# Paged decode attention beside an FFN: five small stages for two score pieces, and another order of buffers, copies and gathers

## The chip, the cores and the metric

The kernel runs on one core of a Trainium2 chip. The metric is the time of one execution on the device in microseconds (us); each kernel is given with the median of several runs. The program uses TensorE (PE in the profile, with PEld for its weight loads), VectorE (DVE), ScalarE (ACT), GpSimd (POOL) and SyncE (SP). SP only issues DMAs; POOL issues the gathers here.

## The reference, cut to what matters

One layer of a hybrid decoder runs over 512 prompt tokens and over 8 sample sequences of 4 new tokens, all with the same weights: an FFN, a mixer (a gated linear recurrence beside latent attention, 4 heads each), and a second FFN.

```python
h = h + 0.5 * rmsnorm(swiglu(rmsnorm(h, norm_g[0]), wg[0], wu[0], wd[0]), norm_g[1])
m, c_kv, k_r, s_fin = mixer(rmsnorm(h, norm_g[2]), ...)
h = h + rmsnorm(m, norm_g[3])
h = h + 0.5 * rmsnorm(swiglu(rmsnorm(h, norm_g[4]), wg[1], wu[1], wd[1]), norm_g[5])
```

The change touches the attention of the sample sequences over their cached keys. A sequence has 4,096 cached positions in pages of 128, which a page table names. A position has a latent row of 256 and a rotary row of 64 floats; the four heads share them. With 4 tokens by 4 heads there are 16 queries for each sequence:

```python
past_c = cache_kv_latent[l][page_table].reshape(Bs, past_len, KV_LORA)
past_r = cache_k_rope[l][page_table].reshape(Bs, past_len, QK_ROPE)
s = (jnp.einsum('bqhr,bsr->bhqs', ql, c_kv) + jnp.einsum('bqhd,bsd->bhqs', qr, k_rope)) * scale
p = jax.nn.softmax(jnp.where(k_pos <= q_pos, s, -jnp.inf), axis=-1)
o = jnp.einsum('bhqs,bsr->bqhr', p, c_kv)
```

## The kernel before

The 544 tokens are two parts: a (256 prompt tokens) and b (256 prompt tokens and the 32 sample tokens). Activations lie with features on the partitions. Every large product is made in three matmuls from a high and a low part of each operand (`gemm` L249, `mm3` L241, which holds L246). `weight` (L219) loads a block of 128 output columns on SP's queue into `wraw`, ACT casts it to the high part `wh` (L237), and DVE subtracts to get the low part `wl` (L238).

The stages in order are: FFN one on both parts, the mixer, and then the stretch that the change touches: the decode attention (the scope "dec", from L1022) interleaved with the second FFN of part a, the generator `gb` (L1019). Behind it come the output projection of part b, its second FFN (`gB`) and the last norms, with the rest of `gb` placed between them by `tail_a` (L1263) and the counts in `FILL` (L54).

`ffn` (L297) has 22 gate and up columns in four chunks; after each chunk it adds the chunk's share of the eight output columns ("down" columns). A unit, the work between two `yield`s, is one gate and up column (48 matmuls of 128x128 by 256 columns for part a) or one down column. There are 22 + 32 = 54 units. The halves `hha` and `hla` are the high and low parts of the chunk's hidden activations, written by ACT and DVE (L158, L159) and read by the down columns.

The decode attention works in 16 halves, two for each sequence (class `Half`, L1075). A half has two blocks of 1,024 cached positions: 1 MB of latent rows and 256 KB of rotary rows each, 8 rows to a partition. The steps of a half are:

- `gather` (L1081): two indirect DMAs on POOL's queue for each block. The latent rows go into one of six slots (`ulb`, `uhb`, `ha`, `hb`, `mb`, `q0`, the names under which the profile shows them), the rotary rows into one of four `rraw` buffers. Both blocks of a half are gathered at once.
- `turn` (L1100): DVE transposes 32x32 squares, three instructions a block (L1105 twice, 128x1024 each, L1106 for the rotary rows), into `kh` of 10 KB a partition, two buffers.
- `score` (L1109): 80 f32 matmuls on small tiles (64 rows by 32 columns) over ten feature columns, in two pieces of five columns (40 matmuls, L1118). They accumulate in two PSUM banks `s`, one for each r. Behind the second piece two reductions (L1125) and a maximum (L1127) give the greatest score of each row.
- `peak` (L1129): a matmul (L1131) spreads the maxima over the partitions; DVE reduces them and makes the bias of the exponential.
- `weigh` (L1138): two Exp on ACT, from PSUM to SBUF, with the row sums.
- `place` (L1143): a DVE transpose, and 16 small copies (32x64, L1149) into `pbuf`, 8 on DVE and 8 on ACT.
- `value` (L1151): 16 f32 matmuls (128 rows by 32 columns, L1157) of the weights with the gathered rows, straight behind the second score piece of a later half. After a sequence's second half the sums are copied to SBUF; `gathered` (L1163) adds up the four partition groups with two matmuls.

`decode` (L1171) puts these steps in thirds of a half: half n is gathered in its own turn, turned in turn n + 1, scored in turn n + 2, and its values follow in turn n + 3. The loop at the end of the scope takes one third, or one unit of `gb`, by a fixed ratio; in this way 43 of the 54 units fall into the decode:

```python
na, nb = NS + (NS + 2) // 3, int((22 + 32) * DRATE)
while ia < na:
    if ia * nb <= ib * na:
        next(ga, None)
        next(gn, None)
        ia += 1
    else:
        next(gb, None)
        ib += 1
```

`decode_new` (L1031) handles the new tokens' own keys between these steps. `decode_end` (L1210) combines the partial sums and makes the last products (L1243 is the matmul of the outputs); it also brings part b's mixer outputs back from DRAM on SP's queue.

PSUM has eight banks: four of tag "acc" for `gemm` and four of tag "ps", taken in turn, for all else (`ps`, L132). The order of the instructions on each engine is the order in which the code issues them.

Of the kernel before, what the change touches and what calls it, by code (L numbers as in the profile page):

```python
# [8 lines left out]
F32 = mybir.dt.float32  # L9
# [8 lines left out]
P = 128  # L18
# [3 lines left out]
NB = 8  # L22
# [27 lines left out]
NPS, PRT = {"ps": 4, "acc": 4, "pr": 1}, "ps"  # L50
# [3 lines left out]
FILL = (4, (7, 8, 9), (1, 2, 3, 4), 4)  # L54
# [5 lines left out]
DRATE = 0.8  # L60
KHB = 2
# [42 lines left out]
def hybrid_step_kernel(  # L104
# [27 lines left out]
    def ps(name, tag="ps"):  # L132
        return pp.tile([P, 512], F32, name=name, tag=tag, bufs=NPS[tag])
# [122 lines left out]
    def gemm_q(wt, act_):  # L256
# [3 lines left out]
        for k in range(kt):  # L260
            if k and k % 2 == 0:
# [35 lines left out]
    def ffn(i, n_post, xs, u, nxt=None, mid=None, late=None, fin=None, pre=()):  # L297
# [5 lines left out]
        for c, (f0, nf) in enumerate(FCH[i]):  # L303
            hh = {x: mk([P, FCH[i][0][1], HS[x]], F32R, "hh" + "ab"[x], pool=pool) for x in xs}
            hl = {x: mk([P, FCH[i][0][1], HS[x]], F32R, "hl" + "ab"[x], pool=pool) for x in xs}
            for j in range(nf):
                f = f0 + j
                wg_ = (w0 or [weight([wcols(w_g[i], 0, KD, f * P)], KD)]).pop(0)
                ga = {x: gemm(wg_, u[x]) for x in xs}
# [3 lines left out]
                up = {x: gemm(wu_, u[x]) for x in xs}  # L313
# [16 lines left out]
            for grp in groups:  # L330
                wts = {d: pre.pop(0) if pre else weight([wcols(w_d[i], f0, nf, d * P)], nf, len(grp) > 1) for d in grp}
                for x in xs:
                    for d in grp:
                        acc = gemm(wts[d], (hh[x], hl[x]))
# [18 lines left out]
                yield  # L353
# [665 lines left out]
    gb = ffn(1, 5, (0,), u4, late=lambda: rstd_u(u4[0], 0), pre=seam)  # L1019
    next(gb)  # L1020

    with scope("dec"):  # L1022
# [44 lines left out]
        slots = ("ulb", "uhb", "ha", "hb", "mb", "q0")  # L1067
# [3 lines left out]
        NS = 3 * NH2 + 11  # L1071

        PTG = {"ulb": 0, "uhb": -1, "ha": -1, "hb": 1, "mb": 0, "q0": -1}

        class Half:  # L1075
            def __init__(self, n):
                self.n, self.b, self.i = n, n // 2, n % 2
                self.bs = slice(self.b * 16, self.b * 16 + 16)
                self.p = pbuf[:, n % 2]

            def gather(self):  # L1081
                self.craw, self.rraw = [], []
                for g in range(2):
                    blk = 2 * self.n + g
                    slot = slots[blk % len(slots)]
                    if slot == "q0":
                        craw = qt
                    else:
                        craw = mk([P, ROWS * R + (256 if g == PTG[slot] else 0)], F32, slot, pool=act)
                    if g == PTG[slot]:  # L1090
                        self.pt = craw[:, ROWS * R :].rearrange("p (a k) -> p a k", a=ROWS)
                    craw = craw[:, : ROWS * R].rearrange("p (a r) -> p a r", a=ROWS)
                    rraw = mk([P, ROWS, RD], F32, "rraw", 4)
                    off = bass.IndirectOffsetOnAxis(ap=idx[:, blk : blk + 1], axis=0)
# [14 lines left out]
            def score(self, js):  # L1109
                q = qbd[self.b % 2]  # L1110
                if js[0] == 0:
                    self.s = [ps("s") for _ in range(2)]
# [319 lines left out]
```

## Time and profile before

| what | value |
|---|---|
| time, median of 3 runs (lowest, highest) | 1321.18 us (1320.61, 1322.22) |
| profiled execution: its own time | 1323.93 us |
| profiled execution: span, instructions | 1322.2 us, 30478 |
| mean granted TensorE clock in it | 0.994 |
| DVE, ACT, POOL busy | 887.5, 697.8, 76.7 us |
| DMA: moved, mean rate | 192.87 MB, 146 GB/s |

The profile is one execution. A busy time is the time in which an engine had an instruction in work. Matmuls overlap and their ends are modelled, so the busy share of PE is an upper bound of its use, and what PE really takes is read from the starts of instructions that follow each other. PEclk is the clock that the throttle granted, as a share of full speed. In a group's row, `out<-in` are the program's names; the last column is the time that the engine stood idle ahead of the group and the instruction that ended most of it ("issue": nothing that the profile shows). An order, shown in the prediction for both kernels, lists instructions of one engine in program order with the number of repeats; it has no times.

### The profile page before, as it was taken

The numbers are of one execution on the slowest core, as the hardware profiler recorded it, in microseconds if no ns is written. First come the engines' busy times: TensorE is split into PE (matmuls) and PEld (weight loads), VectorE is DVE, ScalarE is ACT, GpSimd is POOL, SyncE is SP. The second block draws the span as 40 slices with busy tenths as digits, with TensorE's granted clock in tenths as the row PEclk, the third lists the DMA queues.
The fourth block names the chain that finished last, engine by engine and source line by source line (L and its number), as shares of the span: only waits on it lengthen the run. The fifth ranks groups of instructions, "written<-read, shape, count | busy, mean of one in ns | idle before, by whom it ended". The sixth has DMA issues, their size and how long they took to land.

```text
span 1322.2 us, 30478 instructions
## 1 busy us (share of the span) xinstructions
PE 1284.7 (97%) x12696; PEld 1203.1 (91%) x12696; DVE 887.5 (67%) x1781; ACT 697.8 (53%) x1455; POOL 76.7 (6%) x80
## 2 busy tenths in 40 slices
PE   7999999999999999999999999999899999999998
PEld 6999999999999988889897887887787999999997
DVE  7553245434457787876867788989888868566664
ACT  7543244224456654445747665553455777554454
POOL 0000000000000000000000312313210000000000
PEclk9999999999999999999999999999899999999999
DMA  7223232233253313323332778968768645656451
GB/s 217 88 81 96 81 97 74 86 96 92 77 164 101 109 52 89 90 79 106 84 90 81 285 237 277 302 226 298 265 203 276 170 139 170 174 145 186 139 157 55
DMA packets 280552, 192.87 MB, mean 146 GB/s; under 512 B 12765, under 2 KB 271422, under 8 KB 275550
## 3 DMA queue, kind: packets, MB, share of 16 engines
q1 hardware_dynamic: 271920, 147.65, 38.7%
q0 software_dynamic: 7168, 41.95, 8.3%
q8 instruction: 100, 1.64, 0.5%
q10 hardware_dynamic: 1326, 1.32, 0.3%
q14 instruction: 38, 0.31, 0.1%
HBM read 181.22 MB, written 9.67 MB: 144 GB/s over the span
## 4 chain that ended last, share of the span: by engine, by line
PE 80%; DVE 10%; ACT 5%; issue 3%; DMA 2%; DVEq 0%; SPq 0%; ACTq 0%
PE acc L246 60%; PE acc L264 8%; DVE kh L1105 2%; PE s L1118 2%; DVE wl L238 2%; ACT wh L237 2%; PE s L922 1%; PE o L1157 1%; PE pa L661 1%; DMA wraw<-w_d 1%; PE zx L554 1%; ACT pbuf L1149 1%; DVE ssq L173 1%; PE pr L179 1%; DMA wraw<-w_g 0%
## 5 line engine op out<-in xcount | busy, mean ns | idle before, releaser
L237 ACT CAST wh<-wraw 128x1024 fp32r<-128x1024 f32 (+3 forms) x255 | 248.3, 976 | 318.1 <-PE acc L246 269.5
L238 DVE TENSOR_TENSOR wl<-wraw,wh 128x1024 fp32r<-128x1024 f32 (+3 forms) x255 | 288.3, 1132 | 140.1 <-ACT wh L237 139.4
L246 PE MATMUL acc<-uhb,wh 128*128 128x288 f32 x768 | 227.8, 297 | 0.8 <-ACT uhb L195 0.8
L246 PE MATMUL acc<-ulb,wh 128*128 128x288 f32 x768 | 227.2, 296 | 0.0
L246 PE MATMUL acc<-uhb,wl 128*128 128x288 f32 x768 | 225.7, 295 | 1.2 <-DVE wl L238 1.2
L246 PE MATMUL acc<-uha,wh 128*128 128x256 f32 x768 | 220.2, 287 | 2.1 <-DVE sil L318 1.0
L246 PE MATMUL acc<-uha,wl 128*128 128x256 f32 x768 | 217.2, 284 | 1.3 <-DVE wl L238 1.2
L246 PE MATMUL acc<-ula,wh 128*128 128x256 f32 x768 | 217.6, 284 | 0.6 <-DVE ula L196 0.6
L246 PEld LDWEIGHTS acc<-uha,wh 128*128 128x128 f32 x768 | 145.6, 190 | 6.7 <-issue 3.3
L246 PEld LDWEIGHTS acc<-uha,wl 128*128 128x128 f32 x768 | 145.4, 190 | 2.3 <-DVE wl L238 2.3
L246 PEld LDWEIGHTS acc<-ula,wh 128*128 128x128 f32 x768 | 145.7, 190 | 1.1 <-DVE ula L196 1.0
L246 PEld LDWEIGHTS acc<-uhb,wl 128*128 128x128 f32 x768 | 144.4, 188 | 1.7 <-DVE wl L238 1.7
L246 PEld LDWEIGHTS acc<-uhb,wh 128*128 128x128 f32 x768 | 144.1, 188 | 1.6 <-ACT uhb L195 1.0
L246 PEld LDWEIGHTS acc<-ulb,wh 128*128 128x128 f32 x768 | 144.2, 188 | 0.1
L246 PE MATMUL acc<-hhb,wh 128*128 128x288 f32 x317 | 93.5, 297 | 0.7 <-ACT hhb L158 0.7
L246 PE MATMUL acc<-hlb,wh 128*128 128x288 f32 x317 | 93.9, 297 | 0.1
L246 PE MATMUL acc<-hhb,wl 128*128 128x288 f32 x317 | 92.9, 294 | 0.0
L246 PE MATMUL acc<-hha,wh 128*128 128x256 f32 x297 | 87.4, 294 | 1.1 <-ACT hha L158 1.1
L246 PE MATMUL acc<-hla,wh 128*128 128x256 f32 x297 | 84.5, 284 | 1.1 <-DVE hla L159 1.1
L246 PE MATMUL acc<-hha,wl 128*128 128x256 f32 x297 | 84.5, 285 | 0.2 <-DVE wl L238 0.2
L321 DVE TENSOR_TENSOR sil<-sil,acc 128x256 f32<-128x256 f32 (+1 forms) x88 | 38.1, 435 | 49.7 <-PE acc L246 47.7
L320 DVE TENSOR_TENSOR sil<-sil,sit 128x256 f32<-128x256 f32 (+1 forms) x88 | 38.4, 440 | 45.0 <-ACT sit L295 44.7
(478 smaller groups left out, 2766.1 us busy)
## 6 DMA issues: line engine op xcount, KB each, us to landing
wraw<-w_g SPq DMA_DIRECT2D x66, 512.0 KB
wraw<-w_u SPq DMA_DIRECT2D x66, 512.0 KB
wraw<-w_in SPq DMA_DIRECT2D x24, 512.0 KB
wraw<-w_d SPq DMA_DIRECT2D x32, 384.0 KB
wraw<-w_d SPq DMA_DIRECT2D x32, 320.0 KB
wraw<-w_o SPq DMA_DIRECT2D x16, 512.0 KB
wraw<-w_d SPq DMA_DIRECT2D x16, 448.0 KB
wraw<-w_d SPq DMA_DIRECT2D x8, 512.0 KB
```

What stands on the lines that cost most here:

```text
L173: (eng or nc.vector).tensor_tensor(acc, acc, q, op=ALU.add)
L179: nc.tensor.matmul(pr[:, :n], ones, acc, start=True, stop=True)
L237: nc.scalar.copy(wh[:, :kt], w[:, :kt])
L238: nc.vector.tensor_tensor(wl[:, :kt], w[:, :kt], f32(wh[:, :kt]), op=ALU.subtract)
L246: nc.tensor.matmul(out, a, b, start=n == 0, stop=n == last)
L264: nc.tensor.matmul(acc[:, :n], a[:, k], b[:, k], start=k + i == 0, stop=k == kt - 1 and i == 2)
L320: nc.vector.tensor_tensor(s, s, t, op=ALU.mult)
L321: nc.vector.tensor_tensor(s, s, up[x], op=ALU.mult)
L554: nc.tensor.matmul(z, w[a][:, k], U[1][b][:, k], start=k + n == 0, stop=k == KD - 1 and n == 2)
L661: nc.tensor.matmul(pa[es, c * 32 : (c + 1) * 32].rearrange("p (n m) -> p n m", m=m), kx[:, cs], up(qx[:, cs]), start=True, stop=True, skip ...
L1105: nc.vector.transpose(kh[:, a : a + 4, :8].rearrange("p a j k -> p a (j k)"), self.craw[g][:, a : a + 4])
L1118: nc.tensor.matmul(self.s[r][c * 32 : c * 32 + 32, :P], q[rs, j], kh, start=j == 0, stop=j == 9, skip_group_check=True)
```

## The change

- A half is turned and scored in five stages of two feature columns, `JS`, the two rotary columns first. A stage takes 4 KB a partition in `kh` (three buffers) for both blocks: two DVE transposes of 128x512, and 16 score matmuls.
- The finished scores are copied from PSUM to SBUF (r = 0 by ACT, r = 1 by DVE) straight behind the last stage. One reduction over 128x256 replaces two and a maximum; Exp runs once, in place, from SBUF.
- `peak`, `weigh` and `place` are one step, in the next half's first stage. Of the 16 placing copies 4 are DVE's and 12 ACT's; the transposed weights have buffers of their own (`pt`).
- The values come in two runs of 8 matmuls, one for each block, in stages 3 and 4; behind each run one block is gathered, the rotary rows ahead of the latent rows. There is a seventh slot, `dx`.
- The eight PSUM banks are four "acc", two "ps" that only the scores hold in the decode, one "po" for the values and one "pm" for the maxima; other code takes the last three tags in the turn `CYC`.
- `ffn` with `fine=True` yields twice in each gate and in each up product (every 12 matmuls), and `gemm_2` makes all but the last k step of a chunk's first two down columns, then that step of both (in all chunks but the last). There are now 120 units; 100 of them go into the decode, beside one stage each time in a fixed ratio. `FILL` counts the finer units.
- By the order of SP's instructions the fetches of part b's mixer outputs and of `w_kv` in `decode_end` stand earlier, and two fetches of h later, behind the last values.

```diff
-NPS, PRT = {"ps": 4, "acc": 4, "pr": 1}, "ps"
+NPS, PRT = {"ps": 2, "po": 1, "pm": 1, "acc": 4}, "ps"
+CYC = ("ps", "po", "ps", "pm")
...
-FILL = (4, (7, 8, 9), (1, 2, 3, 4), 4)
+FILL = (13, (7, 8, 9), (1, 2, 3, 4), 4)
...
-DRATE = 0.8
-KHB = 2
+NDEC = 100
+JS = ((8, 9), (0, 1), (2, 3), (4, 5), (6, 7))
+KHB = 3
...
+    def gemm_2(wts, act_):
+        kt = wts[0][2]
+        n = act_[0].shape[-1]
+        accs = [ps("acc", "acc")[:, :n] for _ in wts]
+        for ks in (range(kt - 1), (kt - 1,)):
+            for (wh, wl, _), acc in zip(wts, accs):
+                for k in ks:
+                    for i, (a, b) in enumerate(((wh, act_[0]), (wh, act_[1]), (wl, act_[0]))):
+                        nc.tensor.matmul(acc, a[:, k], b[:, k], start=k + i == 0, stop=k == kt - 1 and i == 2)
+            if len(ks) > 1:
+                yield
+        return accs
...
-                ga = {x: gemm(wg_, u[x]) for x in xs}
+                ga, up = {}, {}
+                for x in xs:
+                    ga[x] = (yield from gemm_q(wg_, u[x], 4)) if fine else gemm(wg_, u[x])
+                if fine:
+                    yield
...
-        slots = ("ulb", "uhb", "ha", "hb", "mb", "q0")
+        slots = ("ulb", "uhb", "ha", "hb", "mb", "q0", "dx")
...
+            def turn(self, st):
+                kh = mk([P, 2, ROWS, 2, 32], F32, "kh", KHB)
+                j = JS[st][0]
                 for g in range(2):
...
+                    src = self.craw[g][:, :, j * 32 : j * 32 + 64] if j < 8 else self.rraw[g]
+                    nc.vector.transpose(kh[:, g].rearrange("p a j k -> p a (j k)"), src)
+                self.kh.append(kh)
...
-                mx = mk([P, 2], F32, "mxd", 2)
                 for r in range(2):
-                    nc.vector.tensor_reduce(mx[:, r : r + 1], self.s[r][:, :P], axis=AX.X, op=ALU.max)
+                    (nc.vector.tensor_copy if r else nc.scalar.copy)(self.e[:, r * P : r * P + P], self.s[r][:, :P])
                 self.mx = mk([P, 1], F32, "mxh", 2)
-                nc.vector.tensor_tensor(self.mx, mx[:, :1], mx[:, 1:], op=ALU.max)
+                nc.vector.tensor_reduce(self.mx, self.e, axis=AX.X, op=ALU.max)
...
-                        (nc.scalar.copy if g % 2 else nc.vector.tensor_copy)(self.p[g * 32 : g * 32 + 32, c // 2, c % 2 * 4 : c % 2 * 4 + 4, self.i * 16 : self.i * 16 + 16], src)
+                        (nc.scalar.copy if g else nc.vector.tensor_copy)(self.p[g * 32 : g * 32 + 32, c // 2, c % 2 * 4 : c % 2 * 4 + 4, self.i * 16 : self.i * 16 + 16], src)
...
+                for st in range(len(JS)):
                     if at(2):
-                        at(2).score(range(5, 10))
-                    if at(3):
-                        at(3).value(H.get(n - 4))
-                    if n >= 3 and at(0):
-                        at(0).gather()
-                    yield
...
+                        at(2).score(st)
+                    if n < 3 and st == 0:
+                        gather(2 + n // 2)
+                    if st == 0 and at(3):
+                        at(3).peak()
+                    if st == 1 and at(4) and at(4).i:
+                        at(4).gathered()
+                    if st >= 3 and at(3):
+                        at(3).value(at(4), st - 3)
+                        gather()
+                    if at(2) or n == 1 and st >= 2:
+                        turn()
                     yield
...
-        na, nb = NS + (NS + 2) // 3, int((22 + 32) * DRATE)
-        ia, ib = 1, 0
-        while ia < na:
-            if ia * nb <= ib * na:
-                next(ga, None)
+        na, ib = len(JS) * (NH2 + 2) + 4, 0
+        for ia in range(na):
+            next(ga)
+            if ia % 2:
                 next(gn, None)
-                ia += 1
-            else:
-                next(gb, None)
+            while ib * na < (ia + 1) * NDEC:
+                next(gb)
                 ib += 1
```

More of the change, by code (lines that the diff above doesn't have):

```diff
@@ L130, in scope, with ps @@
             cur.pop()
-    def ps(name, tag="ps"):
+    turns = [0]
+    def ps(name, tag="ps", own=False):
+        if tag == "ps" and not own:
+            tag = CYC[turns[0] % 4]
+            turns[0] += 1
         return pp.tile([P, 512], F32, name=name, tag=tag, bufs=NPS[tag])
@@ L260, in gemm_q @@
         for k in range(kt):
-            if k and k % 2 == 0:
+            if k and k % step == 0:
                 yield
@@ L312, in ffn @@
                 wu_ = (w0 or [weight([wcols(w_u[i], 0, KD, f * P)], KD)]).pop(0)
-                up = {x: gemm(wu_, u[x]) for x in xs}
+                for x in xs:
+                    up[x] = (yield from gemm_q(wu_, u[x], 4)) if fine else gemm(wu_, u[x])
                 behind[1] = behind[0] if f == 1 else None
@@ L330, in ffn @@
             for grp in groups:
-                wts = {d: pre.pop(0) if pre else weight([wcols(w_d[i], f0, nf, d * P)], nf, len(grp) > 1) for d in grp}
+                if fine and not last and grp[0] == 0:
+                    accs = yield from gemm_2([weight([wcols(w_d[i], f0, nf, d * P)], nf) for d in (0, 1)], (hh[xs[0]], hl[xs[0]]))
+                elif fine and not last and grp[0] == 1:
+                    accs = accs[1:]
+                else:
+                    accs = None
+                wts = None if accs else {d: pre.pop(0) if pre else weight([wcols(w_d[i], f0, nf, d * P)], nf, len(grp) > 1) for d in grp}
                 for x in xs:
                     for d in grp:
-                        acc = gemm(wts[d], (hh[x], hl[x]))
+                        acc = accs[0] if accs else gemm(wts[d], (hh[x], hl[x]))
                         if last and fin and d == KD - 1:
@@ L352, in ffn @@
                         next(ends[-1])
-                yield
+                if not accs or grp[0] == 0:
+                    yield
         if mid:
@@ L1100, in turn @@
-            def turn(self):
-                self.kh = []
-                for g in range(2):
-                    kh = mk([P, ROWS, 10, 32], F32, "kh", KHB)
-                    for a in range(0, ROWS, 4):
-                        nc.vector.transpose(kh[:, a : a + 4, :8].rearrange("p a j k -> p a (j k)"), self.craw[g][:, a : a + 4])
-                    nc.vector.transpose(kh[:, :, 8:].rearrange("p a j k -> p a (j k)"), self.rraw[g])
-                    self.kh.append(kh)
-            def score(self, js):
+                blk = 2 * self.n + len(self.craw)
@@ L1113, in score @@
-                for j in js:
+                if st == 0:
+                    self.s = [ps("s", own=True) for _ in range(2)]
+                for jj, j in enumerate(JS[st]):
                     for c in range(4):
```

127 lines of the change are left out of this document (49 added, 78 removed).

## The prediction

> **What bounds the kernel now.** I read the page first, then busy time by windows, then PE's own timeline and waits, because the first view misleads here.
>
> ```profile
> span 1322.2 us, 30478 instructions
> PE 1284.7 (97%) x12696; PEld 1203.1 (91%) x12696; DVE 887.5 (67%) x1781; ACT 697.8 (53%) x1455; POOL 76.7 (6%) x80
> ```
>
> PE looks full, but the ends of its matmuls are modelled, so time can be lost inside that 97%. The change works on one stage, the paged decode attention that runs beside the second FFN of prompt half a. I take the stretch from 763.18 (first FFN matmul behind the new-key scores) to 1037.05 (L1243). Its rows: everything, then L246 alone (FFN, "acc"), L1118 (scores, "s"), L1157 (values, "o"), each with length and busy time (records) by engine.
>
> ```profile
> 763.18:1037.05 273.87, 259.02 (x4442) 221.91 (x4443) 240.17 (x534) 143.45 (x366) 59.94 (x55) 0.98 0.78 256
> 763.18:1037.05 273.87, 172.78 (x1295) 159.31 (x1295) 0.98 0.78 256
> 763.18:1037.05 273.87, 53.85 (x2560) 39.35 (x2560) 0.98 0.78 256
> 763.18:1037.05 273.87, 34.05 (x512) 15.56 (x512) 0.98 0.78 256
> ```
>
> An f32 score or value matmul leaves two records. What PE really needs is read from start to start. The chain of waits shows dense FFN matmuls (start, duration, count):
>
> ```profile
> 956.23 5.69 PE acc L246 x48
> ```
>
> PE's timeline shows what stands between such runs (start, duration, form, count):
>
> ```profile
> 794.57 0.28 PE L246 MATMUL acc<-hha,wh 128*128 128x256 f32 x1
> 794.78 0.41 PE L1118 MATMUL s<-kh,q 64*32 64x128 f32 x4
> 795.12 0.39 PE L246 MATMUL acc<-hla,wh 128*128 128x256 f32 x1
> 795.34 0.28 PE L246 MATMUL acc<-hha,wl 128*128 128x256 f32 x1
> ...
> 799.49 1.38 PE L1118 MATMUL s<-kh,q 64*32 64x128 f32 x80
> 800.80 1.07 PE L1157 MATMUL o<-ulb,pbuf 128*32 128x256 f32 x16
> 801.68 1.05 PE L1157 MATMUL o<-uhb,pbuf 128*32 128x256 f32 x16
> 802.66 0.38 PE L246 MATMUL acc<-hha,wh 128*128 128x256 f32 x1
> ...
> 849.25 2.47 PE L1118 MATMUL s<-kh,q 64*32 64x128 f32 x160
> 851.65 1.07 PE L1157 MATMUL o<-ha,pbuf 128*32 128x256 f32 x16
> ```
>
> A dense FFN matmul takes 5.69/48 = 0.1185 us. Entering a run of small-tile matmuls costs 0.09 more (794.57 to 794.78), the first step after it 0.10 more (795.12 to 795.34). A score run of 80 records takes 1.31 until the next kind starts, one of 160 takes 2.40: 0.0136 a record and 0.22 for each run. 32 value records take 1.86, the second 16 of them 0.98.
>
> The stretch holds 40 score runs and 16 value runs, with 36 entries from FFN and 41 returns to it. So PE needs 1295 x 0.1185 = 153.5, 2560 x 0.0136 + 40 x 0.22 = 43.6, 36 x 0.09 + 41 x 0.10 = 7.3, 16 x 1.86 = 29.8, and for the other 75 records some 0.1 each, 7.5: together 241.7. It has 273.87, so 32.2 us are lost. Where: first the waits of PE's weight loads in the stretch (total, times, longest).
>
> ```profile
> PEld s L1118 <- issue: 12.7, 13, 2.4
> PEld o L1157 <- issue: 5.8, 21, 0.9
> PEld s L1131 <- DVE mxh L1127: 2.0, 4, 0.8
> PEld acc L246 <- DVE hla L159: 1.5, 2, 0.8
> PEld acc L246 <- ACT hha L158: 1.5, 2, 1.0
> PEld o L1157 <- ACT pbuf L1149: 1.0, 4, 0.3
> PEld acc L246 <- ACT wh L237: 0.8, 2, 0.7
> ```
>
> Then one pause in the timeline, with the next DVE transpose:
>
> ```profile
> 946.24 0.18 PEld L1118 LDWEIGHTS s<-kh,q 64*32 64x32 f32 x15 [2.43 <-issue]
> 946.72 1.25 DVE L1105 STREAM_TRANSPOSE kh<-ulb 128x1024 f32<-128x1024 f32 x1 [0.56 <-PE s L1118]
> ```
>
> Then the instruction queue's packets in 943.5 to 946.5 (packets, MB, share), and two windows with PEclk third from last:
>
> ```profile
> q8 instruction: 1, 0.02, 2.3%
> ```
>
> ```profile
> 900.00:920.00 20.00, 18.87 (x433) 14.04 (x413) 18.36 (x43) 8.13 (x26) 5.23 (x7) 1.00 0.88 304
> 920.00:940.00 20.00, 17.65 (x279) 15.14 (x278) 17.27 (x39) 7.95 (x21) 7.40 (x7) 0.91 0.84 302
> ```
>
> Only 6.8 us (2.0 + 1.5 + 1.5 + 1.0 + 0.8) are waits for named work. The rest, 25.4 us, sits in the dense score and value runs: PE pauses up to 2.43 us although nothing is missing (DVE is itself waiting for those scores), one instruction block arrives during the pause, and the clock is lower in such a window (0.09 x 20 = 1.8 us in the second one). I read it as a burst of short matmuls that outruns the fetch of its instructions: 145 score records ran in 2 us before that pause.
>
> **The change part by part.** First PE's order. A half's end in an FFN column stage before; 40 is one of its two score pieces:
>
> ```order
> L246 MATMUL acc<-uha,wl 128x256
> L1118 MATMUL s<-kh,q_8134 32x128 x40
> L1157 MATMUL o<-mb,pbuf 32x256 x8
> L1157 MATMUL o<-q_8768,pbuf 32x256 x8
> L246 MATMUL acc<-uha,wh 128x256
> ```
>
> The same place after, from one score piece to the FFN behind it:
>
> ```order
> L253 MATMUL acc<-hha,wl 128x256
> L1141 MATMUL s<-kh,q_8134 32x128 x16
> L1174 MATMUL o<-ha,pbuf 32x256 x8
> L253 MATMUL acc<-hha,wh 128x256
> L253 MATMUL acc<-hla,wh 128x256
> L253 MATMUL acc<-hha,wl 128x256
> ```
>
> Scores come in sixteens and values in eights, with 12 to 18 FFN matmuls between them. By the order there are now 81 score runs and 32 value runs, 81 entries and 83 returns. The extra cost lies wholly on PE: 41 x 0.22 = 9.0, 45 x 0.09 = 4.1, 42 x 0.10 = 4.2, and 32 x 0.98 - 29.8 = 1.6: **+18.9 us**. If a run of 32 records is priced from the run of four instead (0.34, plus 28 x (1.31 - 0.34)/76), it takes 0.70, not 0.66: +22. A run that hides its entry would give +15.
>
> What it removes: the bursts. A burst is now 32 + 16 records between FFN runs of 1.4 us and more, so I take the pauses and the slow clock as gone except 1.5 us (bounds 0 and all). The two waits at the FFN's chunk ends (hla, hha: 3.0) go as well, since the first two down columns now run all but their last k step before they need the last column. [...]
>
> What it adds as a wait: the score banks. The DVE rows at a half's end, before:
>
> ```order
> L1105 STREAM_TRANSPOSE kh<-ulb 128x4x256
> L1125 TENSOR_REDUCE mxd<-s 128x1 x2
> L1105 STREAM_TRANSPOSE kh<-ulb 128x4x256
> L1127 TENSOR_TENSOR mxh<-mxd 128x1
> L1106 STREAM_TRANSPOSE kh<-rraw 128x8x64
> ```
>
> And after:
>
> ```order
> L245 TENSOR_TENSOR wl<-wraw,wh 128x768
> L1147 COPY q_8134<-s 128x128
> L1129 STREAM_TRANSPOSE kh<-dx 128x512
> L1149 TENSOR_REDUCE mxh<-q_8134 128x1
> L1129 STREAM_TRANSPOSE kh<-ulb 128x512
> ```
>
> The copy now stands where the reductions stood, and PE's next score run, only 12 FFN matmuls later, needs it and ACT's copy. The durations (busy us, mean ns):
>
> ```profile
> L1105 DVE STREAM_TRANSPOSE kh<-ulb 128x1024 f32<-128x1024 f32 x10 | 12.3, 1232 | 0.6 <-PE s L1118 0.6
> L1106 DVE STREAM_TRANSPOSE kh<-rraw 128x512 f32<-128x512 f32 x31 | 21.4, 691 | 0.0
> L1149 DVE COPY pbuf<-ulb 32x64 f32<-32x64 f32 x48 | 9.2, 191 | 0.8
> L1125 DVE TENSOR_REDUCE mxd<-s 128x1 f32<-128x128 f32 x32 | 7.2, 263 | 0.0
> L1054 DVE COPY q<-b 128x128 f32<-128x128 f32 x1 | 0.3, 283 | 0.0
> L238 DVE TENSOR_TENSOR wl<-wraw,wh 128x1024 fp32r<-128x1024 f32 (+2 forms) x64 | 70.1, 1096 | 10.2 <-ACT wh L237 9.6 <-issue 0.2
> L1149 ACT COPY pbuf<-ulb 32x64 f32<-32x64 f32 x48 | 11.6, 242 | 1.4 <-DVE ulb L1145 0.5
> ```
>
> PE reaches the next score run 12 x 0.1185 + 0.09 = 1.5 us after the last score. If DVE has just begun a 1.1 us weight split, the copy ends at 1.1 + 0.28 = 1.4: just in time. The maximum matmul comes at 1.5 + 0.66 = 2.2; copy, one transpose and the reduction (about 0.4, an estimate from 0.263 for half its width) end at 1.4 + 0.69 + 0.4 = 2.5: 0.3 late at worst, and ACT's copy can be late likewise. I take 0.3 us for each half, 16 x 0.3 = 4.8 (bounds 0 and 1.2 a half). Queued behind these on DVE are the key transposes, which run three pieces ahead of PE, so they do not hold it.
>
> DVE's work hardly moves: 64 transposes of 1.23 and 32 of 0.69 (100.8 us) become 160 of 0.69 (110.6), 64 of the 128 placing copies of 0.19 go to ACT (-12.2), and the copy plus a wide reduction replace two reductions and a small maximum (+0.7): -1.7 on 240.17. ACT gets 64 x 0.242 = 15.5 on 143.45 and stays far from full. The seventh gather buffer and the new order of the gathers on POOL's queue get nothing: key transposes wait for PE alone (0.6 in the row above, and no DMA). If the transposes' waits went whole, 0.6 in this group and 2.2 in all would be the gain. The last chunk gets as many FFN matmuls as before, so FILL 13 is neutral. The turn of PSUM buffers shifts a few rows in other stages: 0, within 1. At the end PE has 79 FFN matmuls between the last value and L1243's successor (9.4 us), half of today's, to cover decode_end; on SP the fetches of h stand behind the last values, and w_o weights behind them, with 156 FFN matmuls (18.5 us) as cover. I take 1 us (0 to 4).
>
> Lost after: 1.8 (pbuf, wh) + 4.8 + 1.0 + 1.5 = 9.1. Sum: 18.9 + 9.1 - 32.2 = **-4.2 us**. Against the profiled execution, 1323.93 us (span 1322.2), that is 1319.7. That execution is 2.75 above the median of the runs, 1321.18; the median falls to 1317.0.
>
> **The rivals.** One, *the score banks hold PE*, slower: if DVE or ACT is behind at every half's end, PE waits 1.2 us a half, 19.2 instead of 4.8: 1317.0 + 14.4 = 1331. It decides from (4.2 + 4.8)/16 = 0.56 us a half. For it: DVE is 240.17/273.87 = 88% busy and the buffers fell from four to two for scores. Against: 1.5 us of cover. Two, *DVE sets the pace*: its work stays 238.5 at 88%, so the stretch stays 272 and the time 1319.5. For it: the transposes' own waits on PE are short (0.6 us in all in the row above). Against: 18.36 of 20 us, 92%, in the window from 900. Three, *the pauses stay*, because they follow the number of matmuls and not their density: 18.5 less about 0.2 for each of the 21 value entries, 14, remain instead of 1.5: 1329.5. [...] Four, *nothing waits*: 9.1 less, 1308.
>
> **How the numbers follow.** The forecast has a chance of 0.50, the rivals 0.20, 0.17, 0.06 and 0.07. Within the forecast the switches (+15 to +22) and the waits (4 to 14) give 1308 to 1325. About 0.2% (2.6 us) is what a measurement of this kernel can tell from no change. Faster: 0.36 of the forecast, 0.07 of four, 0.04 of two, 0.47. Same: 0.12 of the forecast, 0.13 of two, 0.02 of one, 0.27. Slower: 0.02, 0.18 of one, 0.06 of three, 0.26. The range, 1308 to 1331, leaves out the tails of one, three and four.
>
> **What would show it.** Right: some 80 score runs of 32 records at 0.66 us, "issue" waits of scores near zero in length beyond 0.2, PEclk 1.00 throughout the stretch, a stretch about 4 us shorter. Wrong: score runs that start late with DVE or ACT copies of s as releaser (one); PE dense only where DVE is (two); pauses of 1 to 2.4 us on issue inside short runs (three); a run of 32 that takes over 0.8 us, or other stages that move by more than 1 us.

## The result, and the profile after

The changed kernel took 1313.46 us (median of 4 runs, 1312.72 to 1314.48), the kernel before 1321.26 beside it: ratio 0.9941, interval 0.9924 to 0.9958, 7.8 us less. The forecast was 4.2 us less, range 1308 to 1331. One thing has to be said at once, because it decides what may be learned here: the same changed kernel, run again later (e9 below, on chip 3), took 1328.18 us where the kernel before took 1324.05, a ratio of 1.0032 (1.0021 to 1.0044). The chip of the first result is not known. The sections below explain the first result, then what was different when it did not come again.

The profiled execution took 1314.48 us:

```profile
span 1312.7 us, 30501 instructions
PE 1288.4 (98%) x12696; PEld 1196.2 (91%) x12696; DVE 879.7 (67%) x1765; ACT 713.9 (54%) x1503; POOL 73.8 (6%) x80
```

PE is 98% busy where it was 97%, and that again tells nothing. Busy time by windows does, with the same anchors in both kernels: from the matmul that sums the squares for the FFN's norm (it stands in the FFN's first column) to the first output matmul, and from there to the end. Before:

```profile
760.55:1037.05 276.50, 261.60 (x4462) 224.26 (x4461) 242.80 (x537) 145.34 (x369) 61.00 (x56) 0.98 0.78 256
1037.05:1322.20 285.15, 277.40 (x2108) 271.78 (x2107) 184.01 (x293) 167.12 (x297) 1.26 (x1) 1.00 0.52 148
```

After:

```profile
760.64:1029.40 268.76, 265.05 (x4471) 217.72 (x4469) 236.61 (x520) 161.63 (x416) 59.26 (x55) 0.99 0.82 263
1029.40:1312.70 283.30, 277.27 (x2101) 271.10 (x2099) 184.03 (x292) 165.97 (x296) 1.26 (x1) 0.99 0.52 149
```

Up to the first anchor nothing moved (760.55, 760.64). The stretch is 7.7 us shorter, though by the order it now holds 1320 FFN matmuls instead of 1304 (+1.9 us), and seven matmuls of the new keys stand ahead of it (-1.0): 8.6 like for like. Behind it 1.85 are gained, 0.95 of them because 8 FFN matmuls fewer are left. What a run costs, from PE's timeline, one score run alone and one with values behind it:

```profile
880.00 0.28 PE L271 MATMUL acc<-uha,wl 128*128 128x256 f32 x1
880.21 0.67 PE L1141 MATMUL s<-kh,q 64*32 64x128 f32 x32
880.81 0.39 PE L271 MATMUL acc<-uha,wh 128*128 128x256 f32 x1
881.03 0.28 PE L271 MATMUL acc<-ula,wh 128*128 128x256 f32 x1
```

```profile
945.06 0.67 PE L1141 MATMUL s<-kh,q 64*32 64x128 f32 x32
945.65 1.07 PE L1174 MATMUL o<-dx,pbuf 128*32 128x256 f32 x16
946.65 0.39 PE L271 MATMUL acc<-uha,wh 128*128 128x256 f32 x1
946.88 0.28 PE L271 MATMUL acc<-ula,wh 128*128 128x256 f32 x1
```

Entering costs 0.21 - 0.12 = 0.09, a score run 0.60, a value run 1.00, the first step behind it 0.10 extra. All 32 value runs take 1.00, and inside score and value runs no step from one matmul to the next is over 0.25 us; before there were 24 such steps, 18.0 us together (what they are is told behind e8). The waits of PE's weight loads in the stretch:

```profile
PEld acc L271 <- DVE wl L245: 3.2, 4, 2.4
...
PEld pm L1153 <- DVE mxh L1149: 1.3, 3, 0.5
...
PEld o L1182 <- ACT q L1177: 1.1, 1, 1.1
...
PEld acc L253 <- ACT q L1147: 0.4, 1, 0.4
PEld s L1141 <- issue: 0.2, 1, 0.2
...
PEld o L1174 <- ACT pbuf L1165: 0.2, 1, 0.2
```

The pauses on issue in score runs (12.7 before) are gone, the score copies (q L1147) hold PE for 0.4 in all, the chunk-end waits are gone. New is a wait of 2.4 us from 776.97 on for a late weight split (wl L245).

### The profile page after: what moved, and what is told of

Same layout as the page of the kernel before. It is cut to its first block, busy times and chain, and to the rows that moved or that the text cites. A ratio compares the mean times of both kernels' runs of the same rounds, so it can differ in the third digit from the quotient of the medians.

```text
span 1312.7 us, 30501 instructions
## 1 busy us (share of the span) xinstructions
PE 1288.4 (98%) x12696; PEld 1196.2 (91%) x12696; DVE 879.7 (67%) x1765; ACT 713.9 (54%) x1503; POOL 73.8 (6%) x80
## 3 DMA queue, kind: packets, MB, share of 16 engines
q8 instruction: 100, 1.64, 0.5%
## 4 chain that ended last, share of the span: by engine, by line
PE 85%; DVE 6%; ACT 5%; DMA 3%; issue 1%; SPq 0%; DVEq 0%; ACTq 0%
PE acc L253 54%; PE acc L271 16%; PE s L1141 3%; PE o L1174 2%; DVE wl L245 1%; ACT wh L244 1%; PE s L954 1%; PE pa L693 1%; DMA wraw<-w_d 1%; PE acc L282 1%; DMA wraw<-w_u 1%; PE zx L586 1%; ACT pbuf L1165 1%; PE pr L186 1%; PE o L986 1%
## 5 line engine op out<-in xcount | busy, mean ns | idle before, releaser
L245 DVE TENSOR_TENSOR wl<-wraw,wh 128x1024 fp32r<-128x1024 f32 (+3 forms) x255 | 288.7, 1133 | 147.9 <-ACT wh L244 147.4
L271 PE MATMUL acc<-uha,wh 128*128 128x256 f32 x528 | 158.3, 301 | 1.0 <-ACT uha L202 1.0
L271 PE MATMUL acc<-uha,wl 128*128 128x256 f32 x528 | 149.7, 284 | 2.3 <-DVE wl L245 2.3
L271 PE MATMUL acc<-ula,wh 128*128 128x256 f32 x528 | 150.3, 285 | 0.0
L253 PE MATMUL acc<-uha,wh 128*128 128x256 f32 x416 | 117.8, 283 | 0.5 <-DVE sil L343 0.5
L253 PE MATMUL acc<-uha,wl 128*128 128x256 f32 x416 | 117.5, 283 | 0.7 <-DVE wl L245 0.7
L253 PE MATMUL acc<-ula,wh 128*128 128x256 f32 x416 | 117.2, 282 | 0.2 <-DVE ula L203 0.2
L271 PEld LDWEIGHTS acc<-uha,wh 128*128 128x128 f32 x528 | 99.8, 189 | 16.3 <-issue 14.0
L271 PEld LDWEIGHTS acc<-uha,wl 128*128 128x128 f32 x528 | 100.4, 190 | 3.7 <-DVE wl L245 3.2
L271 PEld LDWEIGHTS acc<-ula,wh 128*128 128x128 f32 x528 | 100.5, 191 | 1.1 <-issue 1.0
L253 PEld LDWEIGHTS acc<-uha,wl 128*128 128x128 f32 x416 | 78.3, 188 | 1.1 <-DVE wl L245 1.1
L253 PEld LDWEIGHTS acc<-uha,wh 128*128 128x128 f32 x416 | 78.4, 188 | 0.8 <-DVE sil L343 0.8
```

Source lines behind the costliest of these rows:

```text
L245: nc.vector.tensor_tensor(wl[:, :kt], w[:, :kt], f32(wh[:, :kt]), op=ALU.subtract)
L253: nc.tensor.matmul(out, a, b, start=n == 0, stop=n == last)
```

## The experiments

The theory at first, *the fetch*: PE pauses in dense runs because a burst uses up its instructions faster than the next block arrives. A block is 256 of PE's instructions, by before's profile: 100 packets on the instruction queue, and 25,623 instructions of PE. Rivals: *the density alone* (any longer burst pauses), *the gathers* (two gathers at once cause the pauses), *the vector work* (relief of DVE), and *the cover* (FFN work between a score and what waits for its results). The twelve runs were made on four chips: e1 to e4 on chip 2, e5 to e8 on 9, e9 to e11 on 3, e12 on 11. Each ratio is to runs of the kernel before on the same chip; the ratios of two kernels on different chips can be compared only as far as a chip does to both the same. The other columns are read from the one profiled execution of each kernel, from its last matmul that sums the squares to its first output matmul. Pauses are waits of PE's weight loads over 0.25 us on issue in score and value runs, waits those over 0.25 us for named work in any run.

| kernel | ratio (interval) | stretch, us | pauses, us (longest) | waits, us |
|---|---|---|---|---|
| before | 1 | 276.2 | 14.7 (2.43) | 7.3 |
| after | 0.9941 (0.9924 to 0.9958) | 268.5 | 0 | 5.3 |
| e9, after again | 1.0032 (1.0021 to 1.0044) | 282.3 | 11.1 (0.78) | 4.3 |
| e1, pairs | 1.0026 (1.0014 to 1.0039) | 283.9 | 8.8 (2.5) | 18.4 |
| e3, coarse units | 1.0099 (1.0078 to 1.012) | 290.1 | 13.8 (1.3) | 22.8 |
| e4, halves | 1.0217 (1.0185 to 1.0249) | 306.5 | 21.9 (2.0) | 39.4 |
| e5, one value run | 1.0034 (1.0018 to 1.005) | 284.6 | 6.6 (0.58) | 11.7 |
| e6, copies 8 and 8 | 1.0015 (1.0 to 1.003) | 280.2 | 8.4 (0.62) | 5.2 |
| e7, gathers together | 1.0003 (0.9989 to 1.0016) | 277.5 | 11.2 (0.72) | 2.7 |
| e11, three stages | 0.9968 (0.995 to 0.9986) | 271.8 | 15.1 (1.2) | 3.4 |
| e2, before, fine units | 0.9904 (0.9885 to 0.9924) | 264.0 | 3.8 (0.68) | 10.2 |
| e10, the same, whole | 0.9938 (0.9918 to 0.9958) | 265.6 | 9.3 (2.27) | 8.4 |
| e8, values apart too | 1.0037 (1.0023 to 1.0052) | 279.0 | 16.0 (3.58) | 11.3 |
| e12, paced | 0.9978 (0.9969 to 0.9988) | 270.1 | 0.5 (0.49) | 12.1 |

The work behind the stretch took 277.3 to 279.6 us in all fourteen (from the first output matmul to the last), so the stretch carries the differences.

**The control, e9.** It ran late, and it is told first because e1 and e3 to e7, built from the changed kernel, have to be read beside it and not beside the first result. Its kernel is the changed one, unedited.

> The changed kernel itself, once more, as the control of the kernels built from it: e1 and e5 to e7 came out 8 to 15 us slower than its first runs, and two of them have the same instructions on PE in the same order, with pauses of some 0.5 us inside value runs that its first trace doesn't have. Theory that the edits cost this (gathers together, copies on DVE, values in one run): the first result comes again, 0.9941 +- 0.002, no pause over 0.25 us inside score and value runs. Theory that the pauses come and go with the chip or the run, whatever the edit: 1.000 (0.997 to 1.003), with 10 to 20 such pauses, and the edits of e6 and e7 are then worth nothing against it.

Measured: 1.0032, 14.7 us over the first median, with 21 pauses. The second theory's sign came, a little beyond its range. The stretch:

```profile
760.14:1042.46 282.32, 275.92 (x4469) 221.45 (x4468) 237.72 (x520) 161.61 (x416) 58.61 (x56) 0.99 0.79 252
```

It is 13.8 longer than in the first trace between these anchors (268.5 in the table), with DVE's, ACT's and POOL's work the same. The 32 value runs take 41.8 us instead of 32.0, the score runs 52.9 instead of 50.1: 12.6 of it. One of the ten late value runs, PE and POOL (start, duration):

```profile
814.44 0.14 PEld L1174 LDWEIGHTS o<-hb,pbuf 128*32 128x32 f32 x3 [0.20 <-issue]
...
815.18 0.94 POOL L1120 DMA_INDIRECT ha<-pool_c,idx  x1 [0.30 <-issue]
815.52 0.16 PEld L1174 LDWEIGHTS o<-hb,pbuf 128*32 128x32 f32 x4 [0.59 <-issue]
816.25 0.11 PEld L1174 LDWEIGHTS o<-hb,pbuf 128*32 128x32 f32 x1 [0.57 <-issue]
...
816.96 0.15 PEld L1174 LDWEIGHTS o<-hb,pbuf 128*32 128x32 f32 x3 [0.61 <-issue]
```

PE starts a few instructions every 0.72 us around POOL's issue of a gather. Counted over the stretch, for score and value runs of 16 and more records, "near" when a gather's issue begins from 1.9 us ahead of the run's start to 1.0 behind it:

| trace | near: runs, late by over 0.2 us, us lost | far: runs, late, us lost |
|---|---|---|
| e9 | 51, 15, 13.1 | 60, 2, 0.8 |
| e7 | 51, 15, 12.8 | 60, 1, 0.4 |
| e6 | 46, 16, 12.1 | 65, 1, 0.4 |
| after, first | 48, 2, 0.7 | 63, 2, 0.8 |

So on two chips, in three kernels with the same score and value runs in PE's order, dense runs are late beside gather issues and hardly anywhere else; behind the last gather (987.08 in e9) none of seven value runs is late. All 18 steps over 0.25 us in e9's score and value runs end within 2.5 us behind the start of an issue, where only 40% of all steps in these runs do. In the first trace the same neighbourhood cost next to nothing:

```profile
797.21 0.96 POOL L1120 DMA_INDIRECT ulb<-pool_c,idx  x1 [0.30 <-issue]
...
797.28 1.07 PE L1174 MATMUL o<-uhb,pbuf 128*32 128x256 f32 x16
```

Why is open: the instructions and the order are the same, the issues take the same time (0.95 us), and whether the chip, the loading of the program or the time of the run makes the difference was not tested. That the issue itself does it, and not something that goes with it, is argued from the times; no run took the issues away.

**e1, pairs.** FFN pieces behind every second stage only.

```diff
-            while ib * na < (ia + 1) * NDEC:
+            while (ia % 2 == 1 or ia == na - 1) and ib * na < (ia + 1) * NDEC:
```

> The changed kernel with the FFN pieces issued behind every second stage only, so that two stages stand together: bursts of 64 to 96 score and value records with 24 FFN matmuls between them, where the changed kernel has 32 to 48 with 12. By the order 61 entries instead of 83 and 74 score runs instead of 81. Theory of the fetch (PE pauses when a burst uses up its instructions faster than the next block of 256 arrives, some 4 us after it is asked for): bursts of 96 records are 192 instructions, still under a block, so no pause over 0.6 us inside score runs, and the switches saved are 22 x 0.19 + 7 x 0.15 = 5.2 us: 1308 (1306 to 1311). Theory of the density alone (any burst longer than the changed kernel's brings pauses back, some 0.4 us for each of 37 bursts): 1308 + 15 = 1323 at most, pauses of 0.4 us and more in at least ten score runs. Theory of the vector work (the change helped by what it took from DVE, and PE's runs do not matter): 1313.5.

Measured 1.0026, 3 us over before and no faster than e9 (on another chip). Its waits:

```profile
PEld o L1174 <- ACT pbuf L1165: 4.5, 11, 0.6
...
PEld pm L1153 <- DVE mxh L1149: 3.0, 6, 0.5
PEld s L1141 <- ACT q L1147: 2.9, 5, 1.0
...
PEld s L1141 <- DVE q L1147: 2.0, 4, 0.6
```

The score copies, the maxima and the placed weights are now waited for, 12.4 us where the first trace has 1.9. The 4 us that its expectation gives a block to arrive are an estimate; when a block is asked for no trace shows, and in before blocks that passed in 3.8 us and less ended in a pause, those of 4.4 and more did not (behind e8). The fetch theory forecast 1308 and is wrong as a forecast; the cover is what it left out, and so are 4.4 us of steps beside gather issues, as in e9.

**e3, coarse units**, the change without its dense half pieces.

```diff
-NDEC = 100
+NDEC = 43
-FILL = (13,
+FILL = (4,
-    gb = ffn(1, 5, (0,), u4, late=lambda: rstd_u(u4[0], 0), pre=seam, fine=True)
+    gb = ffn(1, 5, (0,), u4, late=lambda: rstd_u(u4[0], 0), pre=seam)
```

> The changed kernel with the coarse FFN units of before (43 of 54 in the decode, 48 matmuls each for a gate and up column): bursts of 64 to 128 records, 54 entries instead of 83, 68 score runs instead of 81. Theory of the fetch: 128 records are 256 instructions in 2.5 us, at the edge, so few pauses (0 to 4 us in all); switches saved 29 x 0.19 + 13 x 0.15 = 7.5, chunk-end waits back 3.0: 1309 (1307 to 1313). Theory of the density alone: 30 bursts x 0.5 = 15 us of pauses, 1324. Theory of the vector work: 1313.5 + 3 = 1316.5.

Measured 1.0099, 0.0067 over e9 (on another chip): the fine units seem to be worth about that much to the five stages. Waits on pbuf 8.4, on the score copies 8.8.

**e4, halves**, FFN pieces behind every fifth stage (five `kh` buffers, six slots).

> The changed kernel with the FFN pieces issued behind every fifth stage only, with five kh buffers and six slots (the seventh had to make room): 13 bursts of 192 records, 45 entries instead of 83, 58 score runs instead of 81. Theory of the fetch: 384 instructions in some 4.2 us outrun the blocks, as they did before; pauses of 0.7 to 2.4 us in most of the 13 bursts, 10 to 20 us with the lower clock, against 38 x 0.19 + 23 x 0.15 = 10.7 saved: 1313 to 1323, each pause ending about 2.4 us behind the start of an instruction block's transfer. Theories of the gathers and of the vector work: no pauses, 1303.

Measured 1.0217. It paused 21.9 us, as the fetch theory said, but not for its reason: no pause over 0.4 us stands where a block of instructions ends (the count is told behind e8), though five blocks passed in 2.4 to 3.9 us. Of 44 steps over 0.25 us in score and value runs that wait for nothing named, 38 end within 2.5 us behind a gather's issue, and 28 lie in or beside eight stretches of 3.4 us at half the clock. Most of the loss is another thing:

```profile
PEld o L1174 <- ACT pbuf L1165: 34.8, 32, 3.0
```

In 12 of the 16 halves the first value run waits over 1 us for its weights: the chain of peak, exponential, transpose and copies has no FFN work beside it.

**e2 and e10, the kernel before with the fine units alone** (`ffn`, `gemm_q`, `gemm_2` and `FILL` of the changed kernel). Cut to the call and the count, from e10; e2 has 100 in place of 101.

```diff
-    gb = ffn(1, 5, (0,), u4, late=lambda: rstd_u(u4[0], 0), pre=seam)
+    gb = ffn(1, 5, (0,), u4, late=lambda: rstd_u(u4[0], 0), pre=seam, fine=True)
-        na, nb = NS + (NS + 2) // 3, int((22 + 32) * DRATE)
+        na, nb = NS + (NS + 2) // 3, 101
```

> The kernel before with nothing changed but the FFN: the finer units and the first two down columns together, 100 of 120 units in the decode. Its two score pieces of 80 records stay, but 12 FFN matmuls and more now stand between them: bursts of 80 and 112 records, none of 192 (there were six). Theory of the fetch: the long pauses (10 us in six score runs, and most of the rest of the 25 us) go, the two chunk-end waits (3.0) go, DVE then sets the pace (242.8 us of work in a stretch of 276.5): 1321 less 15 to 25, 1296 to 1306, below the changed kernel. Theory of the gathers (pauses come from the two blocks gathered at once): they stay, 1318 to 1321. Theory of the vector work: 1318 to 1321, DVE's work being as before.

> As e2, the kernel before with the fine FFN units alone, but with 100 units in the decode, where e2 came to 99 and so used the preloaded blocks of its last down columns one column off (its output a was changed by that, not its work). Score pieces of 80 records, 15 bursts of 112. If e2's gain belongs to the edit: 0.990 (0.988 to 0.993). If what it gained is a matter of where the 256-instruction boundaries fall: anywhere from 0.990 to 1.003, with long pauses where the 193rd instruction of a block falls into a burst.

Measured 0.9904 (e2) and 0.9938 (e10). e2's output a is wrong, for the reason given in e10's expectation, so e10 is the kernel to go by; it lies outside the range for a gain of the edit alone, and six of its pauses stand at block ends (7.1 us, 1.3 in e2), the second theory's sign. A gain as large as the first result's comes here without stages, copies, slots or another gather order. On chip 3, that of e9, e10's kernel took 1314.33 us, the changed one 1328.18, the one before 1324.05: it beats both there. It was not run beside the first result. It has 35 entries into small-tile runs where the changed kernel has 83. Its waits are the maxima's (7.6 in e2, 5.0 in e10), which are wanted 12 to 24 FFN matmuls behind the last score.

**e5, one value run.**

```diff
-                    if st >= 3 and at(3):
-                        at(3).value(at(4), st - 3)
-                        gather()
+                    if st == 3 and at(3):
+                        at(3).value(at(4), 0)
+                        at(3).value(at(4), 1)
+                    if st >= 3 and at(3):
+                        gather()
```

> The changed kernel with both value runs of a half in stage 3, as one run of 32 records; the gathers stay in stages 3 and 4. Bursts of 64 records at 16 places, the rest as in the changed kernel. Theory of the fetch: 64 records are 128 instructions, far under a block, no pauses; 16 x (2 x 1.00 - 1.86) = 2.2 us saved and one wait may come back, since the second block's weights are wanted a stage earlier (0 to 1.5): ratio to the kernel before 0.9925, 0.0015 below the changed kernel. Theory of the density alone: pauses of 0.3 us at 16 places, 0.9960. Theory of the cover (what the changed kernel gains is FFN work between a score and what waits for its results; any step that comes closer to its source costs a wait): pbuf waits of 0.2 us and more at ten or more of 16 places, 0.9950 to 0.9970.

Measured 1.0034, as e9 (on another chip): the 2.2 us of saved entries do not show. The stage moved nearer cost little on pbuf (1.3).

**e6, copies 8 and 8**, `if g % 2` in place of `if g` in the placing copies.

> The changed kernel with the 16 placing copies as before, 8 on DVE and 8 on ACT. Theory of the fetch and theory of the cover: the same time, 0.9941 +- 0.001, DVE has 12 us more work and slack for it, and waits on pbuf stay under 2 us in all. Theory of the vector work: DVE's 64 copies of 0.19 come back, up to 12 us, 0.998 to 1.003.

Measured 1.0015 where the same time as the first result, 0.9941, was expected, and no more than e9 (on another chip), so the copies moved to ACT bring nothing that shows.

**e7, gathers together**, six slots, both blocks gathered behind the second value run.

```diff
-        slots = ("ulb", "uhb", "ha", "hb", "mb", "q0", "dx")
+        slots = ("ulb", "uhb", "ha", "hb", "mb", "q0")
-                        gather()
+                        gather(2 * (st - 3))
```

> The changed kernel with six slots and both blocks of a half gathered together behind the second value run. Theory of the fetch and theory of the cover: the same time, 0.9941 +- 0.001, and no pause over 0.3 us inside score and value runs. Theory of the gathers (blocks of instructions arrive late while two gathers fill the queues): the pauses of before come back, 8 us and more, 1.000, and waits on key transposes with them.

Measured 1.0003, a little under e9 on another chip. The theory of the gathers expected 8 us of pauses here, and they are there, but e9 has them with the gathers spread as well: nothing shows that the seventh slot or the new order of gathers carries the gain. The changed kernel itself was not run on the chip of e6 and e7.

**e8, values apart**, e10 with the value run moved to the step of the maxima.

> The kernel before with the fine FFN units and, besides, the value run (and the gathers behind it) moved to the step of the maxima, ahead of their matmul: score pieces of 80 records and value runs of 32, each alone between FFN pieces, 50 entries. Theory of the fetch and theory of the cover: no burst above 80 records, so pauses under 3 us in all, and 1.9 us of values and 12 FFN matmuls more between the last score and the maxima, so the waits on mxh (7.7 us with the fine units alone) fall under 2; 15 more entries cost 3.0. Together 4.8 + 7.7 - 3.0 - 5 = 4 to 5 us below the fine units alone (0.9904): 0.987 (0.984 to 0.991). Theory of the vector work: DVE's 243 us set the pace, no gain over the fine units alone, 0.990.

Measured 1.0037 where 0.987 was expected. Waits on mxh are 6.9 all the same, and the long pauses are back, one of them the longest of all:

```profile
977.87 0.18 PEld L1143 LDWEIGHTS s<-kh,q 64*32 64x32 f32 x15 [3.58 <-issue]
```

This led to a count of PE's instructions (weight loads, matmuls and semaphores, in order of time; 25,623 in before). The instruction queue of before's page gives the block (packets, MB, share):

```profile
q8 instruction: 100, 1.64, 0.5%
```

That is 16 KB and 256 of PE's instructions a packet. In the trace of before, all eight pauses over 0.7 us in score and value runs stand behind the 193rd instruction of a block of 256, as if the program were cut there. So do six of e8's seven (the seventh, of 1.06 us, waits for DVE's copy q L1194), and five of e10's seven over 0.6 us (of the others one waits for the exponential, one stands beside a gather's issue). Near such a place a packet can be seen on the instruction queue: in before's stretch the 35 take 1.05 us (median, 0.9 to 2.2), and at the eight pauses PE goes on 2.3 to 2.8 us after the packet's transfer begins (3.5 once, where it took 2.0). I read the pause as what is left of this time when the block in work is used up; no trace shows the fetch itself. In before the eight blocks ahead of pauses passed in 1.8 to 3.8 us; the shortest without one in 4.4. In e10 the six that paused passed in 3.5 to 4.1, in the changed kernel none in under 6.0. An example of e10, with the instruction queue's packet in 918 to 922:

```profile
921.76 0.14 PEld L1143 LDWEIGHTS s<-kh,q 64*32 64x32 f32 x3 [2.27 <-issue]
```

```profile
q8 instruction: 1, 0.02, 1.8%
```

It is no sharp threshold: the transfer doesn't begin at a fixed place in the block (in before 0.0 to 14.7 us after the 193rd instruction of the one ahead), and in e2, e4 and e12 eleven blocks of 2.4 to 4.4 us passed without a pause over 0.4.

With this the 24 steps of before can be told apart (18.0 us):

| where | steps | us |
|---|---|---|
| at a block's end | 8 | 11.8 |
| within 2.5 us behind the start of a gather's issue | 6 | 2.4 |
| in or beside a stretch at half the clock (three of them beside a gather as well) | 9 | 3.4 |
| waiting for named work | 1 | 0.5 |

So steps beside gathers stand in the first trace of before too, only fewer than in e9 (18 there, 9.5 us). The half clock looks like a second price of the long pauses. Before has a granted clock of 0.50 for 3.4 us from 889.58, from 930.54 and from 947.60 on, the last two 1.2 and 1.4 us behind the end of its two longest pauses (2.41 and 2.43). These three stretches and e4's eight each follow 3.4 us in which PE was busy 26 to 57% by the profile (57, 37 and 40% in before). In all fourteen traces no step over 0.25 us in score and value runs falls outside these four rows.

Beside e10's trace e8 lost 5.7 us more at block ends, and its 15 more entries are priced at 3.0.

**e11, three stages** of 2, 4 and 4 columns, one value run.

```diff
-JS = ((8, 9), (0, 1), (2, 3), (4, 5), (6, 7))
-KHB = 3
+JS = ((8, 9), (0, 1, 2, 3), (4, 5, 6, 7))
+KHB = 2
```

> The changed kernel with three stages for each half, of 2, 4 and 4 feature columns (two kh buffers of 8 KB, six slots), and both value runs of a half as one run in the last stage, the two gathers behind it; one FFN piece more beside each stage. By the order 52 entries instead of 83, 51 score runs instead of 81, 16 value runs instead of 32, bursts of 32, 64 and 96 records. Prices: 31 x 0.19 + 30 x 0.15 + 16 x 0.14 = 12.6 us saved. Theory of the fetch: pauses only where a block's boundary falls into a burst of 96, about one in five of 15, 1 to 2 us each, 4 us in all, plus some waits on pbuf and mxh (3 to 6): 1.000 - 0.0059 - 0.003, 0.991 (0.988 to 0.995). Theory of the cover: 24 FFN matmuls between steps are not enough for the weights' chain, 10 us and more of waits on pbuf, mxh and the score copies: 0.996 to 1.003.

Measured 0.9968 where 0.991 was expected, 0.0064 under e9 on its chip: that fits the price of fewer runs, though the edit moved gathers and slots as well. But its two gathers follow each other behind the value run, and of its 17.4 us of steps over 0.25 in dense runs 17.2 lie within 2.5 us of a gather's issue, none at a block's end:

```profile
PEld s L1141 <- issue: 14.5, 27, 1.2
...
PEld o L1174 <- ACT pbuf L1165: 3.6, 8, 0.6
```

**e12, paced**, e10 with its units where no block is short.

```diff
+        pace = [1, 1, 1, 1, 1, 1, 2, 2] + [2, 2, 1, 0] * NH2 + [3, 2, 1, 1, 1, 1, 1]
+        for n in pace:
+            next(ga, None)
+            next(gn, None)
+            for _ in range(n):
+                next(gb)
```

> The kernel of e10 (before with fine FFN units, 100 of them in the decode) with the same steps and units in another pace: two units (24 FFN matmuls) behind each score piece, one behind the maxima, none behind the weights' step, where e10 spreads them evenly, one or two behind any step. So 256 instructions in a row on PE hardly ever hold less than 4.6 us of work (0.4 such blocks expected from the order with the prices of the first trace, 5.7 in e10). Theory of the block (PE pauses where a block of 256 instructions passes in under 4.2 us, at its 193rd instruction; the traces of before, e8 and e10 have all their pauses over 0.7 us there): no pause over 0.7 us at such a place (e10 has five, 7.1 us with the shorter ones), the waits on mxh (5.0 in e10) under 2 as well, short pauses behind gather issues as in e10 (3): ratio 0.987 (0.983 to 0.991). Theory of DVE's pace (its 243 us of work fill a stretch of some 255, so PE waits for key transposes as soon as it runs freely): as e10, 0.993 to 0.995, with waits on kh of 5 us and more. Theory that e10's pauses have nothing to do with blocks: pauses of 1 to 2 us in score runs as before, 0.993 to 0.997.

Measured 0.9978. The block theory's sign came: pauses at a 193rd instruction fell from 7.1 us to one of 0.5. The time did not follow:

```profile
PEld s L1143 <- ACT q L1166: 5.3, 11, 1.1
PEld s L1156 <- DVE mxh L1152: 3.4, 2, 3.2
PEld s L1143 <- DVE q L1194: 2.8, 2, 1.7
PEld s L1143 <- DVE kh L1130: 1.3, 2, 0.8
```

With no unit behind the weights' step, the next half's first score waits for the exponential (q L1166), which the even pace of e10 had covered (1.7). The pauses were a cause, and work ahead of a chain's reader is the other; moving units from one to the other gained nothing here, beside e10 on another chip. DVE's pace is not it (kh 1.3).

## Why the prediction was right, and where not

**The pauses.** The prediction read 25.4 us of loss in dense bursts as instruction fetch and let all but 1.5 go. In the first trace none is left. For the long ones their place, the ends of eight blocks, speaks for the fetch: 11.8 us in before; 2.4 beside gather issues and 3.4 at half the clock were something else, and the rest lies in steps under 0.25 us that were not told apart. Rival three, that pauses stay, gave 1329.5; e9's 1328.18 is that time, but not for the rival's reason: the pauses of e9 follow neither the number of matmuls nor blocks (its shortest passes in 6.0 us) but gather issues. The prediction had no such case: "The seventh gather buffer and the new order of the gathers on POOL's queue get nothing" weighed what waits for a gather, not what happens on PE beside its issue. That is the step that failed for e9. It was luck that the first result was taken where gather issues cost 0.7 us and not 13.1: by e9 alone the forecast of a faster kernel would have been wrong.

**The switches, +18.9.** Too dear. A run of 32 records costs 0.60, not 0.66: its fixed part is 0.60 - 32 x 0.0136 = 0.165, not 0.22. 81 x 0.60 + 32 x 1.00 = 80.6 against the 43.6 + 29.8 put down for before is +7.2, and with the 8.3 for entries and returns +15.5. The dearer price, read from a run of four (+22), was the wrong bound. All score runs together took 50.1 us, not 81 x 0.60 = 48.6: four late ones have the other 1.5, so the switches came to +17.0 with them.

**The score banks, 4.8 of waiting.** Measured 0.4 on the copies and 1.3 on the maxima. 12 FFN matmuls are cover enough there. Rival one did not come in the first trace; in e1 and e3, where bursts join, it did (4.9 and 8.8 on the copies).

**The rest of the loss after.** Of 1.8 for weights and pbuf 1.0 came (pbuf 0.2, wh 0.8 in four waits), and of the tail's 1.0 came 1.1 (q L1177, behind the last value). Not foreseen: the 2.4 us wait for a weight split at the decode's start.

**The sum.** The terms that were too dear (3.4 for the switches, 3.1 for the banks, 1.5 for pauses, 0.8 for weights and pbuf) less the split's 2.4 are 6.4 us; the stretch came 4.4 under the forecast (-8.6 for -4.2). Of the 2.0 between them 1.5 are the four late score runs, 0.5 stays open. The forecast's PEclk of 1.00 did not come either (0.92 in the window from 780 to 800). Chunk-end waits, gathers, slots and copies came as costed in the first trace. DVE's work in the stretch fell by 6.2 us (242.8 to 236.6), not 1.7, and no score run waits for kh. Other stages moved by 0.9 us beside the work that changed sides.

**What the parts are worth.** On chips 2 and 3 the finer FFN pieces alone bring a gain as large as the first result's (e2, e10; without them e3 is 0.0067 worse than e9, across chips). The five stages add entries (83 for 35 in e10), each at a price; what they do with the fine pieces is to make every block long (6.0 us) and so end the long pauses. The copies, the slots and the gathers' order are worth nothing that e6 and e7 could show. How much of the first result's own gain is due to each part is argued, since no part was run beside it.

## What to carry to other kernels

Between two uses of the same small-tile kind on PE, put dense work in small pieces, and make sure of two things at once: that 256 of PE's instructions in a row hold some 6 us of work (behind a block of over 6 us no crossing in these fourteen traces cost over 0.4 us; in before those of 4.4 us and more were enough), and that each chain (score, maximum, weights, values) has its share of that work ahead of its reader. In e12, which took units from one to feed the other, nothing was gained. A gain of half a per cent that rests on pauses should be measured on more than one chip, and more than once, before it is believed.

## What the runs showed of the hardware

All of this is counted in the profiles of before, after and e1 to e12.

PE's instructions came in blocks of 256: before's page has 100 packets, 1.64 MB, on the instruction queue (16 KB each), and its trace 25,623 instructions of PE. In before's stretch 27 of 35 crossings, taken at the 193rd instruction of a block, cost nothing over 0.4 us; the other eight cost 11.8 us. Behind a block that lasted over 6 us no crossing in fourteen traces cost over 0.4 us. One under 4 us mostly cost more in three of them (before, e8, e10; all eight in before), and mostly did not in e2 and e4 (one of nine).

On chips 3 and 9 (e9, e6, e7) PE's short matmuls started only a few instructions every 0.5 to 0.75 us around GpSimd's issue of an indirect DMA, 12 to 13 us in a run. In the first result's trace (after) the same instructions lost 0.7 us beside the issues. The cause is open.
